# First-stage normalization with 97-row broadcasts and whole copies, and a final stage in fixed order with row factors from GpSimd

## The chip, the core and the metric

The kernel runs on one core of one Trainium2 chip. The metric is the device time of one execution in microseconds (us). The engines are TensorE (PE; its weight loads are listed as PEld), VectorE (DVE), ScalarE (ACT), GpSimd (POOL) and SyncE (SP), which issues most of the DMAs. PE works out of SBUF and writes into PSUM, which has eight banks of 128 x 512 floats here.

## What is computed

One decoder block on 512 tokens of width 1024, in float32. The parts that matter here are the first lines and the last:

```
hN = x * rsqrt(mean(x*x) + 1e-6) * norm_g
p  = hN @ w_in                       # 8992 columns, split into many branches
...                                  # mLSTM branch ya, sparse-attention branch yb
merged = sigmoid(g_a) * (ya @ w_branch_a) + sigmoid(g_b) * (yb @ w_branch_b)
x   = x + merged @ w_out
out = x * rsqrt(mean(x*x) + 1e-6) * final_norm_g
```

## The kernel before

**Number format.** Every float32 operand of a product is split in two float32r parts: a high one (written by ACT, in places by POOL) and a low one, the difference, by DVE. A product is three matmuls: high x high, high x low, low x high (`hh`, `hl`, `lh` below). PE is given 3025 matmuls.

**Order.** A planner orders the instructions of each engine, except where the code fixes the order: an engine whose name is in the set `ordered` issues in the order of the code, and so does a single instruction that is wrapped in `keep`. All engines run their queues strictly in order; a waiting instruction holds what is behind it.

**First stage (L291 to L474).** The 512 tokens are four blocks of 128 rows, `xts[0]` to `xts[3]`. `norm_g` is one row, `grow` (L297); a float32 matmul of a row of ones with it spreads it over 128 partitions into two PSUM banks `gB` (L321 to L327). Ahead of these, nine matmuls of a tile of zeros into the bank `idle` are issued (`warm`, L305). For each block:

- `squares` (L347): ACT sums the squares; `factor` (L354): POOL adds epsilon and raises to the power -0.5 (`pow` with `mhalf`), which gives `rs[tb]`. `stats` is both.
- `transposed` (L385): per half of 512 columns, DVE multiplies the block by its factor and by `gB`, and PE transposes it in four pieces into a PSUM bank.
- `high` and `low` (L399, L402): ACT copies the bank to `hTh` (the high part of the transposed, normed input hT), DVE writes the difference to `hTl`.
- `some_of` or `mm3`: 24 matmuls per block against 288 columns of `w_in` ("small" columns: two V branches and the gates), loaded as `sraw` and split into `shi` and `slo` by `small_hi` (ACT or POOL) and `small_lo` (DVE), two of eight row groups at a time.
- `evacuate` (L376): ACT and DVE take the 288 sums out of PSUM.

PE, ACT and DVE are in `ordered` here; PE leaves it at L450, so that blocks 2 and 3 are placed by the planner. On POOL the split of the first two row groups, `small_hi(0, "p")`, is written ahead of the factor of block 1.

**Middle.** The first large product, tokens x 1024 columns of `w_in` for V, is done in Winograd's form (`winograd`, L529): seven products of quarters instead of eight. Its sums of token quarters are made by `token_sums` (L489), eight DVE additions which first rebuild the quarters from `hTh` and `hTl`, in the tile `gate`. Then follow many projections, the attention and the mLSTM, which the change does not touch.

**Final stage (L1369 to L1499).** `merged @ w_out` is again in Winograd's form. `product` issues a quarter product: two blocks of 128 rows, 12 matmuls each, into two banks; `hilo` splits weights. The last four are MS2 and MS3 (banks X, rows 2 and 3 in L and R), MS1 (banks Y: row 2, then row 3 in two halves of 256 columns) and MS4, which adds to the same banks Y and gives rows 0 and 1. "Row" here is a block of 128 tokens, L and R its two halves of 512 columns. For each row:

- `aside` (L1402): ACT copies a bank to `late`, and a POOL DMA adds it to `xo`, which holds x.
- `join` (L1408): DVE adds half a bank to `xo`. `joined` also lets ACT square and sum it and DVE multiply it by `fg` (final_norm_g).
- `part_sum` and `scale_out` (L1418, L1430): the factor is made by ACT (Ln, Exp) and refined by four small DVE instructions; then ACT scales L, DVE scales R, and both are stored.

PE is in `ordered` again from L1388 on; ACT and DVE are not (L1460), so the planner places the steps of the four rows between each other.

Of the kernel before, what the change touches and what calls it, by code (L numbers as in the profile page):

```python
# [62 lines left out]
def build(  # L63
# [227 lines left out]
    with tc.tile_pool(name="ph0", bufs=2, side="right") as p0, tc.tile_pool(  # L291
# [5 lines left out]
        grow = p0.tile([1, D], F32, name="grow", bufs=1)  # L297
        keep(nc.scalar.dma_start(grow, norm_g))
# [3 lines left out]
        dve.memset(f(zero), 0.0)  # L302
        idle = PO()
# [38 lines left out]
        epst = p0.tile([128, 1], F32, name="epst", bufs=1)  # L342
        pool.memset(epst, EPS)
# [10 lines left out]
        def factor(tb):  # L354
            v = p0.tile([128, 1], F32, name="v", tag="v", bufs=4)
            r = p0.tile([128, 1], F32, name="r", tag="r", bufs=4)
            rs.append(r)
            keep(pool.tensor_scalar(v, ssq[:, tb : tb + 1], EPS, None, OP.add))
            if tb == 0:
                keep(pool.tensor_tensor(v, v, ssq[:, NT : NT + 1], OP.add))  # L360
            keep(pool.tensor_tensor(r, v, mhalf[:, 0:1], OP.pow))
            yield

        def stats(tb):
            squares(tb)
            fac = factor(tb)
            next(fac)
            return lambda: next(fac, None)
# [14 lines left out]
        stats(0)()  # L383

        def transposed(tb, banks=None):  # L385
            xt, pts = xts[tb], []
            for hf in range(2):
                hs = slice(hf * 512, hf * 512 + 512)
                dve.scalar_tensor_tensor(xt[:, hs], xt[:, hs], rs[tb][:, 0:1], gB[hf], OP.mult, OP.mult)
                ps = banks[hf] if banks else PT()  # L390
                for k in range(4):
                    kk = hf * 4 + k
                    pe.transpose(ps[:, k * 128 : (k + 1) * 128], xt[:, kk * 128 : (kk + 1) * 128], ident)
                pts.append(ps.rearrange("p (k t) -> p k t", k=4))
            return pts

        blk = [slice(tb * 128, tb * 128 + 128) for tb in range(NT)]

        def high(pts, tb, hf):  # L399
            A(hTh[:, hf * 4 : hf * 4 + 4, blk[tb]], pts[hf], AF.Copy)  # L400

        def low(pts, tb, hf):  # L402
            ks = slice(hf * 4, hf * 4 + 4)
            dve.tensor_tensor(hTl[:, ks, blk[tb]], pts[hf], f(hTh[:, ks, blk[tb]]), OP.subtract)

        def some_of(ps, tb, kind, ks, start=False, stop=False):
            ks = list(ks)
            for k in ks:
                l = (hTl if kind == "lh" else hTh)[:, k, blk[tb]]
                r = (slo if kind == "hl" else shi)[:, k, :]  # L410
                pe.matmul(ps[:, :SW], l, r, start=start and k == ks[0], stop=stop and k == ks[-1])

        first = PP(), PP()
# [10 lines left out]
        low(pts0, 0, 0)  # L424
        low(pts0, 0, 1)
        high(pts1, 1, 0)
        high(pts1, 1, 1)
        small_lo(0)
        small_lo(2)
        low(pts1, 1, 0)  # L430
        low(pts1, 1, 1)
        small_hi(6, "p")
        small_hi(4, "a")
        stats(2)()
        some_of(first[0], 0, "hh", lo4, start=True)
        some_of(first[0], 0, "lh", lo4)
        some_of(first[1], 1, "hh", lo4, start=True)
        some_of(first[0], 0, "hh", hi4)
        some_of(first[0], 0, "lh", hi4)
        some_of(first[1], 1, "hh", hi4)  # L440
        some_of(first[0], 0, "hl", lo4)
        some_of(first[1], 1, "hl", lo4)
        some_of(first[1], 1, "lh", lo4)
        some_of(first[1], 1, "lh", hi4)
        pts = transposed(2)
        small_lo(6)
        small_lo(4)
        some_of(first[0], 0, "hl", (6, 7, 4, 5), stop=True)
        some_of(first[1], 1, "hl", (6, 7, 4, 5), stop=True)
        ordered.discard("pe")  # L450
# [3 lines left out]
        stats(3)()  # L454
        pts3 = transposed(3, (PS(), PS()))
        for tb in (2, 3):
            for hf in range(2):
                high(pts, tb, hf)
                low(pts, tb, hf)
            evacuate(tb - 2, first[tb - 2])  # L460
            pts, before = pts3, last if tb == 3 else None
            last = PP()
            mm3(
                last[:, :SW], lambda k: hTh[:, k, blk[tb]], lambda k: hTl[:, k, blk[tb]],
                lambda k: shi[:, k, :], lambda k: slo[:, k, :], range(ND),
            )
        vq = quarters(vview, ((0, 0), (1, 0)))
        w1 = hilo(vq[0, 0])
        evacuate(2, before)
        stream.fetch()  # L470
        vq.update(quarters(vview, ((0, 1), (1, 1))))
        evacuate(NT - 1, last)
# [16 lines left out]
    def token_sums():  # L489
        a, b, c, d = (gate[:, tb].rearrange("p (k t) -> p k t", k=4) for tb in range(NT))  # L490
        t = dve.tensor_tensor
        hl = lambda k: [f(x) for x in parts[k]]
# [150 lines left out]
    def angles():  # L643
# [68 lines left out]
        "P1": (step,), "t3": (job,), "t2": (job, load), "P2": (step,), "C11": (job, step),  # L712
        "w6": (job,), "P6": (ordered.clear,), "P7": (lambda: next(more, None),), "P4": (lambda: next(turn),), "P5": (lambda: next(turn, None),),
# [594 lines left out]
    with tc.tile_pool(name="fin", bufs=1, reuse_waits="tile") as fp:  # L1308
# [90 lines left out]
        fv = fp.tile([128, NT], F32, name="fv")  # L1399
# [8 lines left out]
        def join(tb, cs, bank):  # L1408
            xv = xo[:, tb, cs]
            dve.scalar_tensor_tensor(xv, bank, 0.5, xv, OP.mult, OP.add)  # L1410
            return xv

        def joined(tb, cs, bank, n):
            xv = join(tb, cs, bank)
            A(junk[:, tb * 2 + n % 2, : cs.stop - cs.start], xv, AF.Square, accum_out=fs[:, tb, n : n + 1])
            dve.tensor_tensor(xv, xv, fg[:, cs], OP.mult)

        def part_sum(tb, n):  # L1418
            v = fb[:, tb : tb + 1]
            if n > 1:  # L1420
                dve.tensor_tensor(fs[:, tb, 0:1], fs[:, tb, 0:1], fs[:, tb, 1:2], OP.add)
            dve.tensor_scalar(v, fs[:, tb, 0:1], 1.0 / D, EPS, OP.mult, OP.add)
# [3 lines left out]
        def left(tb, bank):  # L1426
            joined(tb, L, bank, 0)
            part_sum(tb, 1)

        def scale_out(tb, n, pieces):  # L1430
            part, v, r = fb[:, tb : tb + 1], fv[:, tb : tb + 1], fr[:, tb : tb + 1]
            last = fs[:, tb, n : n + 1]
            A(r, last, AF.Ln, bias=part, scale=1.0 / D)
# [88 lines left out]
```

## Time and profile before

| | us |
|---|---|
| median of 3 runs | 621.82 |
| lowest and highest | 621.22, 622.04 |
| profiled execution | 621.46 |
| its span (first to last instruction or transfer) | 619.7 |

The profile is that of one execution. Its page gives the busy time of each engine, slices of the span, the chain of work that ended last, and the costliest groups of instructions. The trace behind it can be asked for a timeline (start and duration of each instruction in us, engine, line, operation, output tile <- input tiles, shape, number of instructions merged, and in brackets the idle time before it and what ended that), for the waits of an engine in total, and for busy times in given stretches. Almost all instructions carry line 79, that of the helper which issues them, so they are told apart by tiles: `xt` is a block of x, `sq` the squares, `pt`, `pp`, `ps` and `po` PSUM banks, `wh` and `wl` the parts of weights. A matmul's duration includes its pipeline's end, so the spacing of starts tells more than the duration. In a stretch view the last numbers are the granted PE clock, the share of the DMA engines and GB/s.

### The profile page before, as it was taken

To read this page: it belongs to the slowest core of one execution; us is meant where nothing else is said; L and a number is where in the kernel's file an instruction comes from. 1 tells how busy PE (TensorE), PEld (TensorE's weight loads), DVE (VectorE), ACT (ScalarE), POOL (GpSimd) and SP (SyncE) were. 2 spreads that over 40 slices of the span, in tenths; PEclk is the share of its full clock that TensorE was granted. 3 is DMA by queue.
4 is the path that set the end of the run, shared out by engine and by line. 5 is a ranking of instruction groups with operands and counts; after the bars stand their busy time and mean duration, and the time that the engine had idled before them with its cause. 6 is when DMAs were issued, how large, how long until landed. Compare 5 with 4: busy or idle time off the path is not lost.

```text
span 619.7 us, 8625 instructions
## 1 busy us (share of the span) xinstructions
PE 605.0 (98%) x3025; PEld 504.6 (81%) x3025; DVE 494.0 (80%) x962; ACT 343.5 (55%) x644; POOL 55.1 (9%) x114
## 2 busy tenths in 40 slices
PE   7999999999999999999999999999999999999995
PEld 5988888888888878787878887888787878888884
DVE  4799989497587587876967777789898997589986
ACT  5555556555452356556666575565656563434565
POOL 2100000000000002122112212000000000010120
PEclk9999999999999999999999999999999999999998
DMA  7944653502059252223132312432233224891624
GB/s 222 359 136 137 219 155 95 175 20 85 18 142 241 69 137 68 69 70 102 35 85 70 86 42 82 133 102 69 68 103 103 68 91 132 296 248 31 204 51 154
DMA packets 82811, 73.92 MB, mean 119 GB/s; under 512 B 4896, under 2 KB 64452, under 8 KB 82768
## 3 DMA queue, kind: packets, MB, share of 16 engines
q1 hardware_dynamic: 81470, 70.48, 38.0%
q0 software_dynamic: 1152, 2.62, 2.3%
q8 instruction: 24, 0.39, 0.3%
q10 hardware_dynamic: 146, 0.27, 0.1%
q14 instruction: 19, 0.16, 0.1%
HBM read 61.30 MB, written 8.39 MB: 112 GB/s over the span
## 4 chain that ended last, share of the span: by engine, by line
PE 76%; DVE 14%; ACT 3%; issue 3%; DMA 2%; POOL 1%; SPq 0%; POOLq 0%; ACTq 0%; DVEq 0%
PE pp L79 45%; PE ps L79 17%; PE pt L79 10%; PE po L79 3%; DVE u L79 3%; DVE wl L79 2%; ACT wh L79 1%; DMA sraw<-w_in 1%; DVE xo L79 1%; DVE Th L79 1%; DVE num L79 1%; DVE P L79 1%; DMA wr<-w_in 1%; DVE qkl L79 1%; ACT P L79 1%
## 5 line engine op out<-in xcount | busy, mean ns | idle before, releaser
L79 PE MATMUL pp<-hTh,wh 128*128 128x512 f32 (+1 forms) x360 | 142.9, 397 | 0.0
L79 PE MATMUL pp<-hTl,wh 128*128 128x512 f32 (+1 forms) x360 | 139.9, 389 | 0.0
L79 PE MATMUL pp<-hTh,wl 128*128 128x512 f32 (+1 forms) x360 | 139.6, 388 | 0.0
L79 ACT ACTIVATE wh<-wr 128x1024 fp32r<-128x1024 f32 x56 | 59.1, 1058 | 55.8 <-PE pp L79 45.5
L79 PEld LDWEIGHTS pp<-hTh,wl 128*128 128x128 f32 x360 | 67.8, 188 | 13.2
L79 DVE TENSOR_TENSOR wl<-wr,wh 128x1024 fp32r<-128x1024 f32 x56 | 68.1, 1217 | 10.9 <-ACT wh L79 10.8
L79 PEld LDWEIGHTS pp<-hTh,wh 128*128 128x128 f32 x360 | 67.8, 188 | 10.6
L79 PEld LDWEIGHTS pp<-hTl,wh 128*128 128x128 f32 x360 | 67.9, 189 | 9.8
L1035 POOL TENSOR_SCALAR P<-P,st 128x128 f32<-128x128 f32 (+1 forms) x64 | 34.4, 556 | 161.2 <-DVE st L79 126.6
L79 DVE TENSOR_TENSOR wl<-T,wh 128x1024 fp32r<-128x1024 f32 x28 | 33.8, 1221 | 11.3 <-ACT wh L79 11.3
L79 DVE TENSOR_TENSOR ptl<-pt,pth 128x512 fp32r<-128x512 f32 (+1 forms) x64 | 29.9, 485 | 14.5 <-ACT pth L79 14.0
L79 ACT ACTIVATE pth<-pt 128x512 fp32r<-128x512 f32 (+1 forms) x64 | 26.7, 433 | 26.2 <-PE pt L79 14.4
L79 ACT ACTIVATE P<-P,st 128x128 f32<-128x128 f32 (+3 forms) x64 | 35.5, 555 | 10.3 <-DVE st L79 9.9
L79 DVE TENSOR_TENSOR wl<-R,wh 128x1024 fp32r<-128x1024 f32 x28 | 33.7, 1219 | 9.1 <-ACT wh L79 9.1
L79 DVE CUSTOM_DVE_ANT_0 P<-ps,cst 128x128 f32<-128x128 f32 (+3 forms) x64 | 30.5, 486 | 12.5 <-PE ps L79 12.1
L79 DVE SCALAR_TENSOR_TENSOR u<-pp,prm,u 128x511 f32<-128x511 f32 (+2 forms) x48 | 35.6, 742 | 0.4 <-ACT u L79 0.2
L79 ACT ACTIVATE wh<-R 128x1024 fp32r<-128x1024 f32 x28 | 29.3, 1057 | 11.7 <-PE pp L79 4.3
L79 ACT ACTIVATE wh<-T 128x1024 fp32r<-128x1024 f32 x28 | 29.0, 1054 | 11.1 <-PE ps L79 6.4
L79 PE MATMUL ps<-k,Th 128*128 128x256 f32 (+2 forms) x112 | 29.1, 341 | 0.9 <-DVE st L79 0.4
L79 PE MATMUL pt<-cst,P 128*128 128x128 f32 x160 | 28.3, 277 | 1.5 <-DVE ptl L79 1.4
L79 PEld LDWEIGHTS pt<-cst,P 128*128 128x128 f32 x160 | 19.7, 140 | 11.5 <-DVE ptl L79 6.5
L79 PE MATMUL pp<-yah,wh 128*128 128x512 f32 x64 | 25.0, 391 | 0.0
(360 smaller groups left out, 1379.5 us busy)
## 6 DMA issues: line engine op xcount, KB each, us to landing
wr<-w_in SPq DMA_DIRECT2D x44, 512.0 KB, 4.1
R<-w_in SPq DMA_DIRECT2D x24, 512.0 KB, 5.0
gD<-sg SPq DMA_DIRECT2D x16, 256.0 KB, 2.0
s<-gD SPq DMA_DIRECT2D x16, 256.0 KB, 3.0
wr<-w_branch_a SPq DMA_DIRECT2D x8, 512.0 KB, 4.6
R<-w_out SPq DMA_DIRECT2D x8, 512.0 KB, 6.9
vD<-cq SPq DMA_DIRECT2D x8, 256.0 KB, 2.1
wr<-vD SPq DMA_DIRECT2D x4, 512.0 KB, 4.3
```

The lines of the kernel that those rows point to most:

```text
L79: ins = fn(*args, **kw)
L1035: pool.tensor_scalar(pj, pj, st[:, 2, j : j + 1], 1.0, OP.mult, OP.mult)
```

## The change

Three parts.

1. **First stage.** `grow` and `one` become tiles of 128 partitions; norm_g is loaded into partition 96, DVE clears partitions 0 to 95, and the two broadcasts are matmuls of 97 rows. Zero matmuls are added after them (6), after the first half of block 0's transposes (3) and after the second (4, where 2 stood). `stats(1)` is written ahead of `small_hi(0, "p")`, so block 1's factor stands ahead of that split on POOL. The order of the rest is written out for all four blocks, and PE stays in `ordered` until all 96 small matmuls are issued.
2. **Token sums.** A new step `whole` lets ACT copy each transposed bank also to `gate`, unsplit (8 copies of 128x512). `token_sums` then needs four DVE additions, in place. One stream job and the second step of `token_sums` are written after the split of w6, no longer before it.
3. **Final stage.** ACT and DVE go back into `ordered` after the matmuls of MS3, and all steps are written out in a fixed order: each row is joined, squared, its factor made, scaled and stored. The factor is made by POOL (`begin` and `more` add up epsilon and the sums, `factor` raises to -0.5). One of the copies through `late` and a DMA (row 3) is a `join` with -0.5 instead. In rows 2 and 3, and in parts of rows 0 and 1, DVE multiplies by the factor and by `fg` in one instruction (`both`).

```diff
-        grow = p0.tile([1, D], F32, name="grow", bufs=1)
-        keep(nc.scalar.dma_start(grow, norm_g))
+        grow = p0.tile([128, D], F32, name="grow", bufs=1)
+        keep(nc.scalar.dma_start(grow[96:97, :], norm_g))
...
+        dve.memset(grow[:96, :], 0.0)
...
-        one = p0.tile([1, 128], F32, name="one", bufs=1)
+        one = p0.tile([128, 128], F32, name="one", bufs=1)
...
-            pe.matmul(ps, one, grow[:, hf * 512 : hf * 512 + 512], start=True, stop=True)
+            pe.matmul(ps, one[:97], grow[:97, hf * 512 : hf * 512 + 512], start=True, stop=True)
             gB.append(ps)
+        warm(6)
...
+        def whole(tb, hf):
+            q = gate[:, tb // 2 * 2 + hf].rearrange("p (k t) -> p k t", k=4)
+            A(q[:, :, tb % 2 * 128 : tb % 2 * 128 + 128], banks[tb, hf], AF.Copy)
...
+        normed(0, 0)
+        turned(0, 0, PT())
+        warm(3)
+        normed(0, 1)
+        turned(0, 1, PT())
+        stats(1)
         small_hi(0, "p")
-        pts0 = transposed(0)
-        after = stats(1)
-        high(pts0, 0, 0)
+        high(0, 0)
+        high(0, 1)
         small_hi(2, "a")
-        high(pts0, 0, 1)
-        after()
-        warm(2)
-        pts1 = transposed(1, (PP(), idle))
+        warm(4)
+        low(0, 0)
+        normed(1, 0)
+        turned(1, 0, PP())
+        some_of(0, "hh", lo4)
+        normed(1, 1)
+        turned(1, 1, idle)
+        low(0, 1)
+        small_hi(6, "p")
+        high(1, 0)
+        high(1, 1)
+        small_hi(4, "a")
...
+        whole(0, 0)
+        whole(0, 1)
+        stats(2)
...
+        whole(1, 0)
+        whole(1, 1)
+        stats(3)
...
+        for tb in (3, 2):
+            for hf in (1, 0):
+                whole(tb, hf)
+        for tb in (2, 3):
+            some_of(tb, "hh", lo4)
...
     def token_sums():
...
-        t(a, *hl("A21"), OP.add)
-        t(b, a, hl("A22")[0], OP.subtract)
-        t(b, b, hl("A22")[1], OP.subtract)
-        t(c, *hl("A11"), OP.add)
-        t(a, c, a, OP.subtract)
-        t(c, b, c, OP.subtract)
-        t(d, c, hl("A12")[0], OP.add)
-        t(d, d, hl("A12")[1], OP.add)
+        t(a22, a21, a22, OP.subtract)
+        t(a21, a11, a21, OP.subtract)
+        t(a11, a22, a11, OP.subtract)
+        t(a12, a11, a12, OP.add)
...
-        "P1": (step,), "t3": (job,), "t2": (job, load), "P2": (step,), "C11": (job, step),
-        "w6": (job,), "P6": (ordered.clear,), ...
+        "P1": (step,), "t3": (job,), "t2": (job, load), "P2": (step,), "w6": (job, step, job),
+        "P6": (ordered.clear,), ...
...
+        def more(tb, n):
+            v = fb[:, tb : tb + 1]
+            keep(pool.tensor_tensor(v, v, fs[:, tb, n : n + 1], OP.add))
+        def factor(tb, n):
+            more(tb, n)
+            keep(pool.tensor_tensor(fr[:, tb : tb + 1], fb[:, tb : tb + 1], mhalf[:, 0:1], OP.pow))
...
+        ordered.update(("act", "dve"))
...
         product(Y[:1], "MS1", w5, tbs=(0,))
+        join(2, R, Y[0])
+        square(2, R, 1)
+        times(3, L)
+        begin(3)
+        factor(2, 1)
+        for n, cs in enumerate((R0, R1)):
+            product((None, Y[1 + n]), "MS1", w5, tbs=(1,), cs=halves_of[n])
+            join(3, cs, Y[1 + n][:, halves_of[n]])
+            square(3, cs, 1 + n)
+            if n == 0:
+                more(3, 1)
+                scaled(2, L)
+                both(2, R)
+                store(2, R)
+        factor(3, 2)
+        scaled(3, L)
+        both(3, R)
+        store(3, R)
         product(Y[:1], "MS4", w3, False, tbs=(0,))
+        join(0, R, Y[0])
+        square(0, R, 1)
+        product((None, Y[1]), "MS4", w3, False, tbs=(1,), cs=halves_of[0])
+        join(1, R0, Y[1][:, halves_of[0]])
+        square(1, R0, 1)
+        factor(0, 1)
+        more(1, 1)
+        times(1, R0)
+        scaled(0, L)
+        product((None, Y[2]), "MS4", w3, False, tbs=(1,), cs=halves_of[1])
+        join(1, R1, Y[2][:, halves_of[1]])
+        square(1, R1, 2)
+        both(0, R)
+        store(0, R)
+        factor(1, 2)
+        scaled(1, L, nc.scalar)
+        both(1, R1)
+        dve.tensor_scalar(xo[:, 1, R0], xo[:, 1, R0], fr[:, 1:2], None, OP.mult)
+        store(1, R)
```

`normed` and `turned` are the two halves of the old `transposed`; `scaled` is ACT's scaling and its store.

More of the change, by code (lines that the diff above doesn't have):

```diff
@@ L440, in build @@
[L440 to L445, printed above, removed]
+        low(1, 0)
+        low(1, 1)
+        some_of(0, "lh", lo4)
+        some_of(1, "hh", lo4)
+        some_of(0, "hh", hi4)
+        some_of(0, "lh", hi4)
+        some_of(1, "hh", hi4)
+        some_of(0, "hl", lo4)
+        some_of(1, "hl", lo4)
+        some_of(1, "lh", lo4)
@@ L453, in build @@
         nc.sync.dma_start(bng, b_nsa_gate[0].partition_broadcast(128))
-        stats(3)()
-        pts3 = transposed(3, (PS(), PS()))
+        for hf in range(2):
+            normed(2, hf)
+            turned(2, hf, PT())
+        three = idle, PS()
+        for hf in range(2):
+            normed(3, hf)
+            turned(3, hf, three[hf])
+        vq = quarters(vview, ((0, 0), (1, 0)))
         for tb in (2, 3):
             for hf in range(2):
[L458 to L467, printed above, removed]
-        w1 = hilo(vq[0, 0])
-        evacuate(2, before)
+                high(tb, hf)
+                low(tb, hf)
+            if tb == 2:
+                evacuate(0, sums[0])
+        w1 = hilo(vq[0, 0])
+        evacuate(1, sums[1])
+        for tb in (3, 2):
[3 more added lines that the diff above has]
+            some_of(tb, "hh", lo4)
+            some_of(tb, "hl", lo4)
+            some_of(tb, "hh", hi4)
+            some_of(tb, "hl", hi4)
+            some_of(tb, "lh", lo4)
+            some_of(tb, "lh", hi4, stop=True)
+        ordered.discard("pe")
+        evacuate(2, sums[2])
         stream.fetch()
         vq.update(quarters(vview, ((0, 1), (1, 1))))
-        evacuate(NT - 1, last)
+        evacuate(NT - 1, sums[3])
         sp.tile([128, 120], F32, name="pad")
@@ L1406, in aside, with join @@
                 pool.dma_start(xo[:, tb, j * 512 : j * 512 + 512], t, accum_op=OP.add)
-        def join(tb, cs, bank):
+        def join(tb, cs, bank, scale=0.5):
             xv = xo[:, tb, cs]
[L1410 to L1416, printed above, removed]
@@ L1428, in left @@
[L1428 to L1433, printed above, removed]
-            dve.scalar_tensor_tensor(v, last, 1.0 / D, part, OP.mult, OP.add)
-            A(r, r, AF.Exp, scale=-0.5)
-            dve.scalar_tensor_tensor(v, r, v, r, OP.mult, OP.mult)
-            dve.tensor_scalar(v, v, -0.5, 1.5, OP.mult, OP.add)
-            dve.tensor_tensor(r, r, v, OP.mult)
-            for cs, eng in pieces:
-                xv = xo[:, tb, cs]
-                if eng == "a":
-                    A(xv, xv, AF.Copy, scale=r)
-                else:
-                    dve.tensor_scalar(xv, xv, r, None, OP.mult)
-                queue = nc.scalar if eng == "a" and tb == 1 else nc.sync
-                queue.dma_start(out[0, tb * 128 : tb * 128 + 128, cs], xv)
+            join(tb, L, bank)
@@ L1448, in build @@
+            square(tb, L, 0)
+            times(tb, L)
+            begin(tb)
         X = [PS() for _ in range(2)]
@@ L1490, in build @@
-        joined(2, R, Y[0], 1)
-        scale_out(2, 1, ((L, "a"), (R, "d")))
-        list(row(3))
-        product(Y[:1], "MS4", w3, False, tbs=(0,))
-        joined(0, R, Y[0], 1)
-        scale_out(0, 1, ((L, "a"), (R, "d")))
-        last = row(1)
-        for n, cs in enumerate(halves_of):
-            product((None, Y[1 + n]), "MS4", w3, False, tbs=(1,), cs=cs)
-            next(last, None)
+        R0, R1 = slice(512, 768), slice(768, 1024)
+        join(2, L, X[0])
+        square(2, L, 0)
@@ new lines, in build @@
+        A(late[:, 4], X[0], AF.Copy, scale=-0.5)
+        pool.dma_start(xo[:, 2, R], late[:, 4], accum_op=OP.add)
+        times(2, L)
+        begin(2)
+        join(3, L, X[1])
+        w3 = [
+            tuple(wp.tile([128, 2, 512], F32R, name=t, tag=t, bufs=4) for t in ("wh", "wl"))
+            for _ in range(2)
+        ]
+        for (hi, _), q in zip(w3, b22):
+            A(hi, q, AF.Copy)
+        square(3, L, 0)
+        for (hi, lo), q in zip(w3, b22):
+            dve.tensor_tensor(lo, q, f(hi), OP.subtract)
+            if lo is w3[0][1]:
+                join(3, R, X[1], -0.5)
```

112 lines of the change are left out of this document (48 added, 64 removed).

## The prediction

> **What bounds the kernel now.** I read the page's busy shares first, then what TensorE (PE) waited for over the whole span, then the chain of waits at the start.
>
> ```profile
> PE 605.0 (98%) x3025; PEld 504.6 (81%) x3025; DVE 494.0 (80%) x962; ACT 343.5 (55%) x644; POOL 55.1 (9%) x114
> ```
>
> ```profile
> PE pp L79 <- DVE xt L79: 1.8, 1, 1.8
> PE pt L79 <- DVE ptl L79: 1.4, 4, 0.6
> ```
>
> ```profile
> 11.55 1.12 PE pp L79 x4
> ...
> 20.41 0.87 PE pt L79 x8
> ...
> 23.24 6.40 PE pp L79 x48
> 29.63 5.46 PE ps L79 x24
> ```
>
> PE is busy for 98%. Its longest wait is the 1.8 us that ends at 11.55; from there its matmuls follow each other to the last one at 611.90, and the next entry of the list is 1.4 us in four pieces. So the end is: when PE's dense work starts, how fast its first part runs, and the tail behind the last matmul. Work that the change adds to or takes from ScalarE (ACT), VectorE (DVE) or GpSimd (POOL) in between is worth nothing while PE stays fed.
>
> The timeline of the start:
>
> ```profile
> 1.32 2.29 PE L79 MATMUL po<-zero 128*128 128x256 f32 x9 [1.32 <-DVE lfs L79]
> 3.54 3.78 PE L79 MATMUL ps<-grow,one 1*128 1x512 f32 x4
> 6.65 1.06 ACT L79 ACTIVATE sq<-xt 128x1024 f32<-128x1024 f32 x1 [1.55 <-DMA xt<-x]
> 7.25 0.71 PEld L79 LDWEIGHTS pt<-cst,xt 128*128 128x128 f32 x4 [1.50 <-DVE xt L79]
> 8.40 0.60 ACT L79 ACTIVATE hTh<-pt 128x512 fp32r<-128x512 f32 x1 [0.61 <-PE pt L79]
> 9.07 0.68 POOL L336 TENSOR_SCALAR shi<-sraw 128x576 fp32r<-128x576 f32 x1 [2.97 <-DMA sraw<-w_in]
> 9.82 0.22 POOL L358 TENSOR_SCALAR v<-ssq 128x1 f32<-128x1 f32 x1
> 10.13 0.58 POOL L361 TENSOR_TENSOR r<-v,mhalf 128x1 f32<-128x1 f32 x1
> 10.74 1.41 DVE L79 SCALAR_TENSOR_TENSOR xt<-xt,r,ps 128x512 f32<-128x512 f32 x2 [2.58 <-POOL r L361]
> 11.24 0.67 POOL L336 TENSOR_SCALAR shi<-sraw 128x576 fp32r<-128x576 f32 x1 [0.53 <-DMA sraw<-w_in]
> 12.07 1.28 DVE L79 TENSOR_TENSOR hTl<-pt,hTh 128x512 fp32r<-128x512 f32 x2
> 13.17 1.31 PE L79 MATMUL pp<-shi,hTh 128*128 128x288 f32 x4
> 15.24 1.98 PE L79 MATMUL pp<-shi,hTh 128*128 128x288 f32 x8
> 18.12 1.23 PE L79 MATMUL pp<-slo,hTh 128*128 128x288 f32 x8
> 29.47 0.39 PE L79 MATMUL ps<-wh,hTh 128*128 128x512 f32 x1
> ```
>
> Two things are to be seen. First, block 1's squares are done at 7.8, but its factor on POOL stands behind a weight split that waits for a DMA until 9.07; so the factor comes at 10.7 and block 1's transposes at 11.55. Second, the clock: eight matmuls of 288 columns take 1.98 at 15.24 and 1.23 at 18.12, ends included, or 0.25 and 0.133 each (48 in 6.40). PE runs at half clock until about 16.9, though the slices print 9 there. Nine matmuls of zeros and 3.4 us of one-row matmuls did not raise it: the transposes at 7.25 still go at 0.18, against 0.11 (eight in 0.87) at 20.41.
>
> **Part 1, the first stage.** I added it up queue by queue, in program order, with the rows above. The same addition over the order of before gives 29.35 for the first Winograd matmul; measured is 29.47, so I add 0.1.
>
> When does the clock rise? Before, dense full-row work began at 11.55 and the clock rose at 16.9, 5.35 later; counted from the first 288-column matmul it is 3.75. The trace shows no 97-row matmul. If it counts like a full-row one, PE is dense from 1.32 and the clock rises between 5.1 and 6.7; I take 6.7, the longer count. The duration of a 97-row matmul is bounded by the one-row rows, 0.86 at half clock, and half of that: 3.54 to 6.96. The new clearing of `grow`, 96x1024, lies between a 0.38 memset of 384 columns and about 1.1 scaled up; it ends by 2.4, hidden before 3.54. If it had to wait for norm_g's landing, it would cost up to 1.0.
>
> Then: six warm matmuls at 0.12 to 7.7 (0.4 later than the transposes at 7.25, the price of the filling), block 0's transposes and three more to 8.9. On POOL block 1's factor now stands ahead of the split: squares end 7.8, factor 8.7. ACT copies block 0's banks 8.35 to 9.75, shi[2:4] to 10.3; DVE does block 0's first low part 9.0 to 9.7, then block 1's product to 10.3. Block 1's transposes start at 10.36 (11.55 before) and the first sums at 10.8 (13.17). PE waits once more, 12.8 to 13.2, for shi[4:6], which ACT makes after block 1's copies. From there 36 matmuls x 0.133 = 4.8 to 18.0; 16 transposes 1.75 plus 0.4 of waits for block 3's factor to 20.2 (ACT makes the squares of 2 and 3 between the new whole copies); 48 x 0.133 = 6.4 to 26.6. With the 0.1: 26.7 against 29.47, **2.75 gained**. The weights of that product are split on DVE by 25.8, so they wait for nothing. The eight whole copies (0.5 each) and the evacuations end by 28.3, beside PE. The loads of the three bias rows keep their place ahead of the weight quarters on SP, so no transfer moves. Of the 2.75, some 1.2 is the earlier start of block 1 and the rest the clock.
>
> **Part 2, the token sums.** Eight DVE additions become four:
>
> ```profile
> L79 DVE TENSOR_TENSOR gate<-gate,hTl 128x1024 f32<-128x1024 f32 x2 | 2.4, 1224 | 0.0
> ```
>
> Some 4.7 us of DVE go. PE had no wait there, so I cost it at 0; what it buys is cover for the start that now comes 2.75 earlier. The job moved behind w6 leaves PE's order of products and jobs the same.
>
> **Part 3, the end.**
>
> ```profile
> 603.52 0.87 POOL L1406 DMA_DIRECT2D xo<-late  x1 [2.13 <-ACT late L79]
> 604.58 0.68 DVE L79 SCALAR_TENSOR_TENSOR xo<-pp,xo 128x512 f32<-128x512 f32 x1
> 606.40 0.40 PE L79 MATMUL pp<-wh,mSh 128*128 128x512 f32 x1
> 606.87 0.42 DVE L79 SCALAR_TENSOR_TENSOR xo<-pp,xo 128x256 f32<-128x256 f32 x1 [1.60 <-DMA xo<-late]
> 611.90 0.28 PE L79 MATMUL pp<-wh,mSl 128*128 128x256 f32 x1
> 612.23 0.42 DVE L79 SCALAR_TENSOR_TENSOR xo<-pp,xo 128x256 f32<-128x256 f32 x1
> 613.15 0.42 ACT L79 ACTIVATE junk<-xo 128x256 f32<-128x256 f32 x1
> 614.40 0.30 ACT L79 ACTIVATE fr<-fs,fb 128x1 f32<-128x1 f32 x1
> 615.60 0.72 ACT L79 ACTIVATE xo<-xo,fr 128x512 f32<-128x512 f32 x1 [0.67 <-DVE fr L79]
> 616.35 0.38 ACTq L1446 DMA_DIRECT2D out<-xo  x1
> ```
>
> PE's last matmul ends at 612.18; the last scaling ends at 616.32, 4.14 later. The old factor takes from the last square, 613.66 with its accumulator read, to 615.60: 1.94 over two ACT and four DVE instructions. The new one is two POOL instructions; the first stage has their like:
>
> ```profile
> 5.25 0.19 POOL L360 TENSOR_TENSOR v<-v,ssq 128x1 f32<-128x1 f32 x1 [0.74 <-ACT sq L79]
> 5.51 0.58 POOL L361 TENSOR_TENSOR r<-v,mhalf 128x1 f32<-128x1 f32 x1
> 6.13 0.75 DVE L79 SCALAR_TENSOR_TENSOR xt<-xt,r,ps 128x512 f32<-128x512 f32 x1 [4.84 <-POOL r L361]
> ```
>
> 0.88 from the first to the reader, about 1.0 with the hand-over. But the fixed order puts each row's scaling ahead of the next row's join on DVE and ACT, so the four factors stand in one chain. From PE's own times: block 2's square ends 605.9, factor 606.9; DVE does block 2's scaling, then block 3's last join, 607.6 to 608.0, one us after its bank was full; square, factor 609.5; block 3's scaling, block 0's join to 610.8; factor 612.6; ACT scales block 0 to 613.3 while block 1's last join (612.8) waits; its square ends 613.75, factor 614.75, last scaling 615.5 on ACT and 615.4 on DVE. That is **0.85 before** 616.32. The stall at 606.87 goes with its DMA (block 3's part is a DVE join, 0.7). PE keeps its cover: block 2's last join ends at 605.2 and the second low weight at 604.6, both needed from 606.40 on, where the last products begin to add to the same banks. Bounds: POOL rows vary by 0.1, four in the chain, so 0.4 to 1.2.
>
> At these times POOL's power for row 0 (611.7 to 612.6) meets DVE's product by `fg`, both operands in SBUF. The Trainium skill, "SBUF — State Buffer", "Who interferes with whom", says that such a DVE instruction and a GpSimd one that reads SBUF shut each other out; no row here shows it. By it the sum would be about 0.2 poorer.
>
> **Sum.** The profiled execution took 621.46 (span 619.7 and 1.8 around it): 621.46 - 2.75 - 0.85 = 617.9. The median of the runs, 621.82, lies 0.36 above the profiled one; I say 618.0. Its own range: rise at 5.1 gives 0.6 more, at 8.1 0.65 less, the end 0.4 either way: 616.9 to 618.9.
>
> **Rivals.**
> - *Late rise.* The 97-row matmuls do not count as full; dense work begins at 6.96, and 5.4 later the clock rises, at 12.4. Everything to there runs at 0.25 and 0.18. First product at 28.35: 1.1 gained, 619.5. For it: one-row matmuls did nothing. Chance 0.17.
> - *The clock falls again.* From 6.7 to 13.5 PE has about 1.4 us of waits and four groups of four transposes. At the end of the run the clock fell 2.1 us after the last matmul (mean 0.63 in this slice, and 0.50 after it):
>
> ```profile
> 614.00:615.00 1.00, 0.00 (x0) 0.00 (x0) 0.74 (x5) 0.90 (x3) 0.00 (x0) 0.63 0.00 0
> ```
>
> My longest wait is 1.0, so I expect no fall; but if a third of idle time is enough, it falls at 10.1 and rises at 16.9 as before: first product at 28.9, 0.6 gained, 620.0. Chance 0.13. The Trainium skill, "TensorE: Matmul & The Clock Gate", "Part 4: PE-mode transpose", says that transposes do not count as PE-busy; by it this stretch would be busy for only 55%, and this rival is what it would give. The same page, "Part 1", has the clock rise after some 3.4 us of sustained work whatever it is; the trace disagrees, since PE was busy from 1.32 to 8.8 without a rise.
> - *It does not do what it says*: the clock rises at 16.9 as before. Filling and half clock eat the earlier start, 29.5 against 29.47; only the end is left: 620.6. Chance 0.10.
> - *Slower: the chain of four powers.* Each factor is waited for by DVE and ACT in order, so a factor longer by d moves the end by 4d. It eats its own gain from d = 0.2; the whole is slower by 1.24 (0.2%) from d = (2.75 + 0.85 + 1.24)/4 = 1.2. At d = 1.3 it gives 617.9 + 5.2 = 623.1. For it: POOL never made these beside a busy DVE in a trace shown here. Against it: its last DMA issue is over by 601.4, and 0.58 is a steady row. Chance 0.08, with every other way to lose.
>
> **How the numbers follow.** Forecast 0.52, late rise 0.17, fall 0.13, no rise 0.10, slower 0.08. Down to 620.4 the range leaves out the last two, 0.18. A measurement of this kernel tells about 0.2%, 1.24 us, from no change: faster 0.82, same 0.10, slower 0.08.
>
> **What would show it.** Right: 288-column sums at 0.133 from the first one on; block 1's transposes near 10.4; first Winograd matmul near 26.7, last matmul near 609.4; no PE wait in between; the last scaling 3.3 after the last matmul. Wrong: sums at 0.25 before 16.9; a PE wait behind `grow`; a PE wait in the last products for a join; factors over 1.1 in the tail.

## The result and the profile after

The changed kernel takes **618.03 us** (median of 6 runs, 617.80 to 618.76) against 621.53 for the kernel before on the same chip (6 runs, 620.70 to 622.04): a ratio of 0.9946, 95% interval 0.9934 to 0.9959. A second set of 5 runs gave 618.08 and the same ratio and interval (experiment 9). The forecast was 618.0. The profiled execution took 617.8, with a span of 615.78.

The busy shares of the page after, and what PE waited for (total, times, longest):

```profile
PE 602.1 (98%) x3036; PEld 502.7 (82%) x3036; DVE 488.5 (79%) x932; ACT 345.9 (56%) x643; POOL 59.3 (10%) x126
```

```profile
PE pp L79 <- DVE xt L79: 0.8, 1, 0.8
```

PE issues eleven matmuls more than before and is yet busy for 2.9 us less, since fewer of its matmuls run at half clock; the wait of 1.8 ahead of block 1 is now 0.8. The timeline of the start:

```profile
3.40 3.14 PE L79 MATMUL ps<-grow,one 97*128 97x512 f32 x4
5.97 1.28 PE L79 MATMUL po<-zero 128*128 128x256 f32 x6
7.09 0.60 PE L79 MATMUL pt<-cst,xt 128*128 128x128 f32 x4
8.20 0.57 POOL L362 TENSOR_TENSOR r<-v,mhalf 128x1 f32<-128x1 f32 x1
9.06 0.68 POOL L339 TENSOR_SCALAR shi<-sraw 128x576 fp32r<-128x576 f32 x1 [0.29 <-DMA sraw<-w_in]
9.76 0.66 PE L79 MATMUL pp<-cst,xt 128*128 128x128 f32 x4 [0.81 <-DVE xt L79]
10.17 0.78 PE L79 MATMUL pp<-shi,hTh 128*128 128x288 f32 x4
25.98 0.40 PE L79 MATMUL ps<-wh,hTh 128*128 128x512 f32 x1
```

The first four sums take 0.78, ends included, where before 0.25 each was seen until 16.9: PE is at full clock. In the trace's clock records it rises at 5.94 (16.93 before). Block 1's factor (8.20) stands ahead of the split (9.06), so its transposes start at 9.76 (11.55 before) and the first Winograd matmul at 25.98 (29.47 before). The tail:

```profile
608.32 0.28 PE L79 MATMUL pp<-wh,mSl 128*128 128x256 f32 x1
608.53 0.55 POOL L1454 TENSOR_TENSOR fr<-fb,mhalf 128x1 f32<-128x1 f32 x1
609.12 0.72 ACT L79 ACTIVATE xo<-xo,fr 128x512 f32<-128x512 f32 x1 [0.53 <-POOL fr L1454]
609.75 0.40 ACT L79 ACTIVATE junk<-xo 128x256 f32<-128x256 f32 x1
610.65 0.55 POOL L1454 TENSOR_TENSOR fr<-fb,mhalf 128x1 f32<-128x1 f32 x1
611.23 0.72 ACT L79 ACTIVATE xo<-xo,fr 128x512 f32<-128x512 f32 x1 [1.00 <-POOL fr L1454]
611.64 0.35 DVE L79 TENSOR_SCALAR xo<-xo,fr 128x256 f32<-128x256 f32 x1
611.99 0.40 ACTq L1457 DMA_DIRECT2D out<-xo  x1
```

Row 0's factor releases ACT at 609.12, ACT's square of row 1 has to wait behind that scaling until 609.75, and so on to the last scaling, which ends at 611.99. From the start of the last matmul this is 3.67; before it was 616.32 - 611.90 = 4.42. The stores of the two ends, issue to landing (median for SP's seven, the one of ACT's queue), first of the kernel before, then of the changed one:

```profile
out<-xo SPq DMA_DIRECT2D x7, 256.0 KB, 2.2
out<-xo ACTq DMA_DIRECT2D x1, 256.0 KB, 2.5
```

```profile
out<-xo SPq DMA_DIRECT2D x7, 256.0 KB, 2.5
out<-xo ACTq DMA_DIRECT2D x1, 256.0 KB, 2.8
```

So the span splits like this:

| stretch | before | after | gain | forecast |
|---|---|---|---|---|
| start to first Winograd matmul | 29.47 | 25.98 | 3.49 | 2.75 |
| from there to the last matmul | 582.43 | 582.34 | 0.09 | 0 |
| last matmul's start to the end of the last scaling | 4.42 | 3.67 | 0.75 | 0.85 |
| from there to the end of the span | 3.36 | 3.79 | -0.43 | 0 |
| outside the span | 1.78 | 2.02 | -0.24 | 0 |
| sum (profiled executions) | 621.46 | 617.80 | 3.66 | 3.60 |

The sum came out within 0.06, and that closeness is luck, because two errors cancel: the start gained 0.74 more than forecast, and the last three rows gave 0.77 less. The 0.24 outside the span is not the end's doing: the time of a run less its span is about 2.0 in every run of the changed kernel and about 1.8 in those of the kernel before, but also 1.8 in the runs of experiments 2 and 7, which have the new end. What makes it is open.

**How the clock moves.** From rise to fall the clock records of the two profiles show 614.26 - 16.93 = 597.33 and 613.51 - 5.94 = 607.57 us, 175.0 and 178.0 times 3.4133, and in all 14 profiles such times are whole numbers of this step. So the clock is decided at the points of a grid of 3.4133 us, which lies differently against the kernel's start in each execution. The Trainium skill, "TensorE: Matmul & The Clock Gate", "Part 1", describes such a free-running window of 3413 ns; the trace agrees, and it fits that the runs of one kernel spread by 1.0 us (after) or 2.7 us (before, 620.32 to 623.04 over 24 runs).

### The profile page after: what moved, and what is told of

It is laid out like the page before. It is cut to its first block, busy times and chain, and to the rows that moved or that the text cites. A ratio compares the mean times of both kernels' runs of the same rounds, so it can differ in the third digit from the quotient of the medians.

```text
span 615.8 us, 8634 instructions
## 1 busy us (share of the span) xinstructions
PE 602.1 (98%) x3036; PEld 502.7 (82%) x3036; DVE 488.5 (79%) x932; ACT 345.9 (56%) x643; POOL 59.3 (10%) x126
## 4 chain that ended last, share of the span: by engine, by line
PE 76%; DVE 14%; ACT 4%; issue 2%; DMA 1%; POOL 1%; SPq 0%; POOLq 0%; DVEq 0%; ACTq 0%
PE pp L79 44%; PE ps L79 18%; PE pt L79 10%; PE po L79 3%; DVE u L79 3%; DVE wl L79 2%; ACT wh L79 1%; DVE P L79 1%; ACT P L79 1%; DMA xt<-x 1%; DVE xo L79 1%; DVE ptl L79 1%; DVE Th L79 1%; DVE num L79 1%; DMA wr<-w_in 1%
## 5 line engine op out<-in xcount | busy, mean ns | idle before, releaser
L79 ACT ACTIVATE wh<-R 128x1024 fp32r<-128x1024 f32 x28 | 29.3, 1058 | 16.2 <-PE pp L79 6.5
```

The costliest lines, as they stand in the source:

```text
L79: ins = fn(*args, **kw)
```

## The experiments

Twelve runs. "Rise" is the clock record's first rise; "tail" runs from the last matmul's start to the end of the last scaling; ratios are to the kernel before on the same chip.

| run | rise | first Winograd matmul | tail | median (range) | ratio, 95% interval |
|---|---|---|---|---|---|
| before | 16.93 | 29.47 | 4.42 | 621.53 (620.70 to 622.04) | |
| after | 5.94 | 25.98 | 3.67 | 618.03 (617.80 to 618.76) | 0.9946 (0.9934 to 0.9959) |
| 1 one row | 11.20 | 28.05 | 3.66 | 620.30 (620.19 to 620.74) | 0.9977 (0.9968 to 0.9986) |
| 2 no filling | 5.48 | 26.38 | 3.66 | 618.63 (617.63 to 619.60) | 0.9956 (0.9941 to 0.9971) |
| 3 old end | 6.34 | 26.57 | 5.28 | 619.43 (619.11 to 619.63) | 0.9963 (0.9950 to 0.9976) |
| 4 joins first | 7.63 | 26.78 | 3.03 | 617.83 (617.65 to 618.28) | 0.9941 (0.9926 to 0.9956) |
| 5 split first | 4.80, 15.04 | 29.13 | 3.66 | 621.15 (619.92 to 622.38) | 0.9992 (0.9982 to 1.0003) |
| 6 slow factor | 7.53 | 26.73 | 5.05 | 619.48 (619.17 to 619.89) | 0.9975 (0.9965 to 0.9985) |
| 7 eight sums | 7.48 | 26.42 | 3.65 | 618.64 (618.37 to 619.30) | 0.9962 (0.9948 to 0.9976) |
| 8 rows only | 17.88 | 30.18 | 4.41 | 621.44 (620.35 to 622.52) | 0.9998 (0.9988 to 1.0008) |
| 9 changed again | 5.12 | 26.14 | 3.65 | 618.08 (617.75 to 618.66) | 0.9946 (0.9934 to 0.9959) |
| 10 joins again | 7.55 | 26.75 | 3.03 | 617.96 (617.37 to 618.07) | 0.9941 (0.9927 to 0.9955) |
| 11 65 rows | 5.12 | 26.43 | 3.65 | 619.21 (618.18 to 619.23) | 0.9960 (0.9945 to 0.9975) |
| 12 end only | 17.74 | 30.14 | 3.65 | 621.26 (620.59 to 622.26) | 0.9997 (0.9988 to 1.0006) |

In the profiles with the new start, 16.2 us pass from block 1's first transpose to the first Winograd matmul (17.52 in run 5, where the clock falls, and 15.93 in run 7, which has no whole copies); in those with the old start, 17.9 to 18.0. What else differs between the profiles with the new start lies ahead of that transpose.

### 1: the changed kernel with a one-row broadcast

```diff
-            pe.matmul(ps, one[:97], grow[:97, hf * 512 : hf * 512 + 512], start=True, stop=True)
+            pe.matmul(ps, one, grow[:, hf * 512 : hf * 512 + 512], start=True, stop=True)
```

> The changed kernel with the broadcasts back to one row (norm_g in partition 0, no clearing). Theory (a matmul of one row does not count for the clock, one of 97 rows does): the clock no longer rises near 6 us but only after full-row work from about 7 us on, between 10.3 and 13.7; the first 288-column sums go at 0.25 each; first Winograd matmul at 27.6 to 28.8 instead of 26.0; 1.2 to 2.2 us slower than the changed kernel. Rival (the added zero matmuls raise the clock, the rows do not matter): rise near 6 us as in the changed kernel, and the same time within 0.4.

Its timeline:

```profile
3.53 3.78 PE L79 MATMUL ps<-grow,one 1*128 1x512 f32 x4
7.24 1.65 PE L79 MATMUL po<-zero 128*128 128x256 f32 x6
8.69 1.05 PE L79 MATMUL pt<-cst,xt 128*128 128x128 f32 x4
9.39 0.99 PE L79 MATMUL po<-zero 128*128 128x256 f32 x3
10.18 1.05 PE L79 MATMUL pt<-cst,xt 128*128 128x128 f32 x4
11.81 0.66 PE L79 MATMUL pp<-cst,xt 128*128 128x128 f32 x4
```

Here four transposes still take 1.05; the clock rises at 11.20, and only block 1's go in 0.66. It costs 2.3 us against the changed kernel. The grid lies almost as in run 4: a window from 4.37 to 7.79 here does not raise the clock, one from 4.21 to 7.63 there does, with 97-row matmuls in it. So the one-row matmuls, busy as they look, leave the clock down, and the 97-row ones bring it up. The window that raised the clock here, 7.79 to 11.20, holds some 1.4 us of transposes (8.69 to 9.39, 10.18 to 10.89). Without them it would be busy for 59%. The Trainium skill, "TensorE: Matmul & The Clock Gate", "Part 4: PE-mode transpose", says that transposes do not count as PE-busy in the same way. Either they do count here, or 59% of a window is enough. No run settles which: the 65% of a window that raised nothing (11.05 to 14.47 in run 8, shown there) are mostly transposes themselves.

### 2: the changed kernel without the added filling

```diff
-        warm(6)
...
-        warm(3)
...
-        warm(4)
+        warm(2)
```

> The changed kernel without the added zero matmuls (6 and 3 taken out, 2 instead of 4), 97 rows kept. Theory (the rows raise the clock; gaps shorter than 2 us do not lower it): rise between 5 and 8 us, no fall, 288-column sums at 0.133 from the first on, block 0's transposes up to 0.7 earlier; first Winograd matmul within 0.4 of 26.0, time within 0.5 of the changed kernel. Rival (without filling the clock falls again): sums at 0.25 between 10 and 13.5 or 17, first Winograd matmul at 27.5 or later, 1.5 to 2.5 slower.

The runs fall into two groups: 617.63, 617.79 and 617.98, and 619.28, 619.28 and 619.60. The profile (617.98) is of the first: clock up at 5.48, and it stays up over a PE wait of 1.93 us, in a grid window that is busy for 63% (the columns are explained under run 5):

```profile
8.89:12.31 3.42, 2.16 (x18) 2.16 (x19) 3.42 (x6) 2.09 (x4) 1.73 (x3) 1.00 1.04 333
```

That the other three lost the clock in a window that held more of the wait fits two of them by the mean granted clock listed for each run (619.28 at 0.995, 619.28 at 0.993; the first group has 0.997 and 0.998). It does not fit the third, 619.60 at 0.997; a later first rise would, as the time ahead of the first rise is listed as 1.00. No profile of any of the three was taken. So the filling costs nothing where the grid is kind, and is worth some 1.5 us where it is not; by which of the two ways is not shown.

### 5: block 1's factor behind the split again

```diff
-        stats(1)
         small_hi(0, "p")
+        stats(1)
```

> The changed kernel with block 1's squares and factor put back behind the weight split of GpSimd that waits for a DMA (as the kernel before has it); the 97 rows, the filling and the end stay. If the earlier place of block 1's factor is worth what the prediction says (1.2 of the 2.75 us): block 1's transposes at about 10.9 to 11.5 instead of 9.76, the first Winograd matmul at about 27.1, the time 0.8 to 1.2 above the changed kernel's 618.0, so 619.0. Rival, the place is worth nothing because PE waits anyway at 12.65 for ScalarE's part of the weights: first Winograd matmul at 26.0 to 26.3, time 618.0 to 618.3. The clock should rise at its first grid point after 4.7 in either case.

Measured 621.15, 3.1 above the changed kernel; both forecasts were far off. The stretch view by the grid of this execution (length, busy time of PE, PEld, DVE, ACT, POOL with counts; then granted clock, DMA share, GB/s; it prints 1.00 also ahead of the first rise):

```profile
4.80:8.21 3.41, 3.04 (x19) 2.21 (x18) 1.41 (x2) 1.90 (x5) 0.76 (x2) 1.00 1.10 299
8.21:11.63 3.42, 0.78 (x8) 0.58 (x6) 1.51 (x3) 1.37 (x3) 1.78 (x4) 1.00 1.14 319
11.63:15.04 3.41, 3.41 (x15) 3.39 (x16) 3.12 (x5) 1.06 (x2) 0.37 (x1) 0.50 0.37 126
15.04:18.45 3.41, 3.41 (x26) 3.25 (x26) 2.03 (x3) 3.41 (x8) 0.52 (x2) 1.00 0.99 378
```

```profile
PE pp L79 <- DVE xt L79: 2.6, 1, 2.6
```

PE waits 2.6 us for block 1, the window 8.21 to 11.63 is busy for only 0.78 of 3.42, and the clock falls for the whole next window, although PE is fully busy in it. That is the rival "the clock falls again", for want of the earlier factor. The factor's place is worth 29.13 - 25.98 = 3.15 in this execution: 1.85 of transposes that start later (11.61 against 9.76), and 1.3 of half clock behind them. Not every execution has the fall. Three of the ten runs (619.92, 620.25 and 620.36) list a mean granted clock of 0.997, and a window at half clock (0.003 of the run) beside the half clock at the run's end (0.0015 or more in every profile) would leave 0.996 at most. They are still 1.9 to 2.3 above the changed kernel, about what the later transposes cost.

### 8: the kernel before with the 97-row broadcast alone

```diff
-            pe.matmul(ps, one, grow[:, hf * 512 : hf * 512 + 512], start=True, stop=True)
+            pe.matmul(ps, one[:97], grow[:97, hf * 512 : hf * 512 + 512], start=True, stop=True)
```

> The kernel before with nothing changed but the 97-row broadcast of norm_g (and its cleared rows). If the row count alone brings the clock: rise at a grid point between 4.7 and 8.2, block 1's transposes at about 11.5 as before, the sums at 0.133 from the first one on; if the clock stays up over the waits before 11.55 the first Winograd matmul is at about 27.2 to 27.7 instead of 29.47 and the time 1.8 to 2.2 below the kernel before. Rival, without filling the clock falls again in the waits of 8 to 11.5: sums at 0.25 at first, first Winograd matmul at 28.5 to 29.4, time 0 to 1 below before. Which of the two comes may hang on where the grid lies, so that single runs spread over both.

With it go the tiles of 128 partitions and the clearing of `grow`, as in the change. Nothing was gained: 621.44 against 621.46, ratio 0.9998 (0.9988 to 1.0008). The grid window 4.23 to 7.64 did not raise the clock, though PE is listed as busy for 3.37 of its 3.41:

```profile
4.23:7.64 3.41, 3.37 (x7) 1.25 (x6) 1.27 (x2) 1.15 (x5) 1.00 (x3) 1.00 0.97 304
...
11.05:14.47 3.42, 2.23 (x10) 2.23 (x11) 3.03 (x5) 0.82 (x2) 1.03 (x2) 1.00 0.58 218
```

```profile
7.06 1.98 PE L79 MATMUL pt<-cst,xt 128*128 128x128 f32 x8
12.24 1.12 PE L79 MATMUL pp<-cst,xt 128*128 128x128 f32 x4 [2.77 <-DVE xt L79]
```

PE's starts leave some 0.24 us free between the broadcasts and the transposes at 7.06, and the matmuls have 97 rows of 128. Then it waits for block 1, and the next chance is a window that begins after 12.24. So in this execution the rows alone do not bring the clock, and over ten runs they gain nothing; in the changed kernel the six zero matmuls close that gap, and the earlier factor the next one. The parts of the first stage do not add up. By the first Winograd matmul in one profile each, the rows without the rest gain nothing (30.18 against 29.47), the rest without the rows 1.4 (28.05), all together 3.5 (25.98).

### 11: 65 rows instead of 97

```diff
-            pe.matmul(ps, one[:97], grow[:97, hf * 512 : hf * 512 + 512], start=True, stop=True)
+            pe.matmul(ps, one[:65], grow[:65, hf * 512 : hf * 512 + 512], start=True, stop=True)
```

> The changed kernel with norm_g broadcast over 65 rows instead of 97; filling, order and end stay. If any count of rows well above one is full work: clock up by 8.2, first Winograd matmul at 25.9 to 26.9, time 617.7 to 618.8 as with 97 rows. Rival, a window's work is weighted by its rows and the clock wants some 0.77 of a full window (the one profile with 97 rows and 0.24 us of idle time, 0.74 by that weight, did not rise; 0.79 and more did): 65 rows give 0.51 to 0.80, so in most executions the clock rises one window later, at 8.3 to 11.7, first Winograd matmul at 27.2 to 28.1, time 619.3 to 620.4, near that of the one-row kernel.

One run took 618.18, as with 97 rows; its profile has the rise at 5.12, in a window half of which were full-row matmuls. The other three took 619.20 to 619.23, above every one of the 11 runs with 97 rows (617.75 to 618.76). So the number of rows still matters between 65 and 97. A weight by rows fits all profiles: full-row time plus 97/128 or 65/128 of the rest makes 0.74 of the window that did not raise the clock in run 8, 0.75 of the one that did here, and 0.79 in run 3. But it rests on two profiles close to the limit, and no profile was taken of the three late runs, so it is not settled.

### 6: one more GpSimd instruction ahead of each power

```diff
+            v = fb[:, tb : tb + 1]
+            keep(pool.tensor_scalar(v, v, 1.0, None, OP.mult))
             keep(pool.tensor_tensor(fr[:, tb : tb + 1], fb[:, tb : tb + 1], mhalf[:, 0:1], OP.pow))
```

> The changed kernel with one further GpSimd instruction of 128x1 (a multiplication by 1.0, about 0.2 busy and 0.3 with its hand-over) ahead of each row's power in the end. If the four factors stand in one chain: the piece from the start of the last matmul to the end of the last scaling grows from 3.63 by about 1.2, or the last matmul comes later by a part of it, and the time is about 619.2. Rival, only the last factor counts because the others have slack behind PE: that piece grows by 0.3, time 618.3.

```profile
612.50 0.22 POOL L1455 TENSOR_SCALAR fb<-fb 128x1 f32<-128x1 f32 x1
612.81 0.57 POOL L1456 TENSOR_TENSOR fr<-fb,mhalf 128x1 f32<-128x1 f32 x1
613.41 0.72 ACT L79 ACTIVATE xo<-xo,fr 128x512 f32<-128x512 f32 x1 [1.33 <-POOL fr L1456]
613.81 0.34 DVE L79 TENSOR_SCALAR xo<-xo,fr 128x256 f32<-128x256 f32 x1
```

The power starts 0.31 later than it could (612.50 to 612.81). The tail grows from 3.67 to 5.05, by 1.38: four times 0.31 and a little, not once. The time follows, 619.48. The four factors do stand in one chain.

### 3 and 12: the old end behind the new start, and the new end behind the old start

Run 3 is the changed kernel with the final stage of the kernel before, of which the core is:

```diff
-        ordered.update(("act", "dve"))
...
-            keep(pool.tensor_tensor(fr[:, tb : tb + 1], fb[:, tb : tb + 1], mhalf[:, 0:1], OP.pow))
...
+            A(r, last, AF.Ln, bias=part, scale=1.0 / D)
...
+        aside(X, 2, 1, 1, -0.5)
```

> The changed kernel with the final stage of before. Theory (end and start are worth 0.8 and 2.7 to 3.5, and simply add): start as in the changed kernel, 4.4 us from the last matmul's start to the end of the last scaling instead of 3.6, 0.5 to 1.1 us slower than the changed kernel. Rival (the end's gain is eaten by what follows the last scaling): the same time within 0.3.

It lost 1.4 us against the changed kernel; the tail is 5.28, not 4.42:

```profile
604.80 0.42 DVE L79 SCALAR_TENSOR_TENSOR xo<-pp,xo 128x256 f32<-128x256 f32 x1 [2.46 <-DMA xo<-late]
```

In the kernel before this wait for the adding DMA was 1.60. The wait is longer by 0.86, as is the tail. The last adding transfer ran for 2.40 us here (602.05 to 604.45 in the transfer records) and for 1.52 there. One of its 144 packets, begun at 602.64, took 0.86 us, where no other took more than 0.24; the last six then come late, one behind the other. What held that packet is not shown; a load of 16 KB of instructions had run from 601.02 to 602.50. The new end has no such transfer in row 3. Without the 0.86 the loss would be some 0.5 us, an estimate that takes all five runs to have it; one was profiled.

Run 12 is the kernel before with the new final stage, the same diff the other way round.

> The kernel before with the new end alone. If the end is worth its 0.85 on its own: tail 3.6 to 3.7 instead of 4.41, 0.7 to 0.9 below the kernel before less 0.4 for the last store's landing in the profile, so 620.7 against 621.5. Rival, behind the late first stage the joins meet the adding transfers in other places and nothing is gained: 621.3 to 621.6. The first Winograd matmul stays at 28.9 to 30.2.

The tail is 3.65, as in the changed kernel, so the end does the same behind either start. But the time is 621.26, ratio 0.9997 (0.9988 to 1.0006): no gain that these runs can tell, though the interval leaves room for up to 0.7 us, and the median of the kernel before in this set is 621.84. Part of the gain goes behind the last scaling. In the three profiles with the old end, 3.36 us pass from there to the end of the span; in those with the new end, 3.67 to 3.90. The transfer records show where: counted from the end of the last scaling, SP's last packet of the kernel before lands at 1.46 and the store of ACT's queue runs nearly alone, 0.84 long, to 2.14; in the changed kernel both halves are stored at 612.0, SP's packets run to 2.21, and ACT's store takes 1.28, to 2.39. Of the 0.43, 0.25 is thus two stores side by side. DVE's half used to be done at 616.08, 0.24 ahead of ACT's; the new end gives DVE two instructions there (611.24 and 611.64), so it ends with ACT's. No kernel was run that stores it sooner, so this cause is read from the records alone.

### 7: the eight token sums again

```diff
-        whole(0, 0)
-        whole(0, 1)
...
-        t(a22, a21, a22, OP.subtract)
+        t(a, *hl("A21"), OP.add)
+        t(b, a, hl("A22")[0], OP.subtract)
+        t(b, b, hl("A22")[1], OP.subtract)
...
```

> The changed kernel with the eight additions of halves (high and low parts) of the kernel before instead of the whole copies and four additions in place. The prediction costs this part at 0: from the first Winograd matmul to the last matmul 582.3 to 582.6 as in every kernel so far, first Winograd matmul 25.7 to 26.4 (ScalarE has eight copies less), time 617.7 to 618.4. Rival, the 4.7 us of VectorE that the four additions save carry the earlier start: PE waits for a sum behind the first products and the middle grows by 1 to 2.5 us, time 619 to 620.5.

Neither side: the middle grew to 583.09, by 0.7 against the changed kernel's 582.34, while the first Winograd matmul came 0.3 earlier than in runs with the same rise (26.42 against 26.73 and 26.75), since ACT has eight copies less. Half of it is one wait:

```profile
42.07 2.35 DVE L79 TENSOR_TENSOR wl<-R,wh 128x1024 fp32r<-128x1024 f32 x2
43.34 0.50 PE L79 MATMUL pp<-wl,hTh 128*128 128x512 f32 x1 [0.19 <-DVE wl L79]
```

DVE splits this weight behind its last additions, at 42.07, and PE, which could start at 42.99, waits until 43.34. In the changed kernel DVE is at that weight at 39.50, and PE does not wait:

```profile
39.50 2.35 DVE L79 TENSOR_TENSOR wl<-R,wh 128x1024 fp32r<-128x1024 f32 x2
```

So part 2 is cover, worth about 0.4 net by these profiles; the medians differ by 0.6, with intervals that overlap. Not all of the middle's growth need be part 2's: the middle is 582.84 and 582.85 in runs 1 and 5, which have part 2, mostly because one wait for DVE (tile `st`) takes 0.75 there instead of 0.40.

### 4, 9 and 10: a version with two joins ahead of a scaling

```diff
             if n == 0:
                 more(3, 1)
-                scaled(2, L)
-                both(2, R)
-                store(2, R)
+        scaled(2, L)
+        both(2, R)
+        store(2, R)
         factor(3, 2)
```

> The changed kernel with row 2's scalings (L on ScalarE, R on VectorE, and the store) written behind row 3's last join and square. Theory (the four factors stand in one chain because each row's scaling waits for its power ahead of the next row's join): row 3's factor comes about 0.9 earlier, row 0's join no longer waits for row 3's scaling, and the last scaling ends 3.0 after the start of the last matmul instead of 3.6: 0.5 to 0.7 faster than the changed kernel. Rival (the tail hangs on the last matmul alone): no change within 0.3.

> The changed kernel itself, beside the next one on the same chip: 617.7 to 618.8, median 618.1; the clock up by 8.2 and no fall, the tail (start of the last matmul to the end of the last scaling) 3.65.

> The changed kernel with row 2's scalings and store moved behind row 3's last join and square. In a single profile the tail was 3.03 instead of 3.66. If the tail decides: 0.6 below the changed kernel, so 617.5 with a tail of 3.0, and the interval of the one lies below the median of the other. Rival, row 2's later store keeps the queue of the stores busy and gives the gain back behind the last scaling: time as the changed kernel, 617.9 to 618.2.

The tail is 3.03 in both profiles, 0.64 less, as expected from taking one scaling out of the chain. The time moves less: 617.96 beside 618.08 in the same set, 617.83 in the first; the intervals (0.9927 to 0.9955 and 0.9934 to 0.9959) overlap, so the two are not told apart. Both profiles of this version have a late rise (7.55 and 7.63, the first Winograd matmul 0.6 to 0.8 later than in the changed kernel's two profiles), and 0.1 goes behind the last scaling again (3.86 and 3.90 to the end of the span). It beats the kernel before; that it beats the changed one is not shown.

## Why the prediction was right, step by step

- **What bounds the kernel.** Right. From the first Winograd matmul to the last, 582.2 to 583.1 us pass in every profile, whatever was done at the two ends.
- **Part 1, the rise of the clock.** The likeliest case came true: matmuls of 97 rows bring the clock and those of one row do not (run 1), with a gap or fewer rows as the limit (runs 8 and 11). The step that failed is the size: the rise was put at 6.7, from two lengths of dense work in one profile, 5.35 and 3.75. There is no such length. The clock is decided on the grid, and profiles of kernels with the whole start of part 1 rise between 5.12 and 7.63. Behind block 1's transposes the addition held: 16.3 to the first Winograd matmul was forecast (10.36 to 26.7), 16.2 was measured. Of the extra gain of 0.74, 0.60 lies ahead of them, as they start at 9.76. In runs 4, 6 and 10, with the rise at 7.53 to 7.63, they start at 10.51 to 10.56 and the first Winograd matmul comes at 26.73 to 26.78, as forecast; so much of the extra gain is luck of where the grid lay. The rise alone does not fix it either: at 5.12 (run 9) the first Winograd matmul comes at 26.14, later than at 5.94. That the trace disagrees with a rise after sustained work of any kind stands, for one-row matmuls (run 1). The free-running window that the Trainium skill, "TensorE: Matmul & The Clock Gate", "Part 1", describes was not used in the forecast, and the two profiles' 175.0 and 178.0 steps agree with it.
- **Part 1, the place of block 1's factor.** The forecast took 1.2 of the 2.75 for the earlier start and the rest for the clock, as if they could be added. The profile after has 1.79 (11.55 to 9.76) and 1.70 (17.92 to 16.22 behind it). But run 5 shows that they cannot be had one by one: with the factor back, the clock falls in its profile, and 3.15 of the 3.49 are gone. Run 8 shows it from the other side. "The price of the filling", 0.4 on block 0's transposes, was not paid in the profile, where they start at 7.09 (7.25 before); with a rise at 7.53 they start at 7.85, so the price hangs on the grid.
- **Part 2.** Costed at 0, with the remark that it is cover for the earlier start. Right: nothing in the middle moved, and without it the wait appears (run 7).
- **Part 3.** The tail gained 0.75 for 0.85, and the chain of four factors is real (run 6). What failed is a term that the prediction put at nothing without a reason: what follows the last scaling. It grew by 0.43, of which two stores side by side are 0.25. How much of the end's gain reaches the clock is not settled: alone it gained nothing that can be told (run 12, at most 0.7), and taking it back behind the new start cost 1.4, 0.86 of it by a slower transfer (run 3).
- **Rivals.** *Late rise* and *does nothing* did not happen; run 1 is what the first would have been (620.3 measured, 619.5 forecast). *The clock falls again* shows in none of the 11 runs of the changed kernel (at most 618.76), but it is near: run 5 has it, and two of run 2's slower three fit it. *The chain of four powers* is right as a mechanism and 4d as its price; d stayed at 0, as the powers took 0.55 to 0.58 as before. The 0.2 that the prediction estimated from the Trainium skill, "SBUF — State Buffer", "Who interferes with whom", for DVE and GpSimd shutting each other out did not show in the tail of the changed kernel. In the tail of runs 4 and 10 one addition on GpSimd, beside a DVE product of two SBUF tiles, takes 0.43 instead of 0.19.

## What to carry to other kernels

Before a change that is to bring the clock up earlier, list the windows of the clock's grid that it could fall on, and look for the one with the least work: here the wider matmul gained nothing alone, and with the filling and the earlier operand 3.5 us. Undo parts of such a change one at a time before any of them is called useless. And follow an end's gain to the landing of the last store: two halves that finish at the same time can share what one of them had to itself.

## What the runs showed of the hardware that was not expected

- The clock's grid of 3.4133 us holds inside a kernel as well: in run 5 it rises at 4.80, falls at 11.63 and rises at 15.04, two and one steps apart. A window does not have to be idle for a fall: those with 39% (the end of the kernel before) and 23% (run 5) of PE work were followed by half clock, those with 46% (the end of run 7) and 63% (run 2) were not.
- A matmul's listed busy time does not tell how it counts for the clock. Windows listed as busy for 99% or more did not raise it, once mostly of one-row matmuls (run 1, 4.37 to 7.79) and once of 97 rows with 0.24 us free between starts (run 8).
- DVE and GpSimd held each other up where both read SBUF. In the changed kernel two splits on DVE meet one on GpSimd:

```profile
10.88 1.89 DVE L79 TENSOR_TENSOR slo<-sraw,shi 128x576 fp32r<-128x576 f32 x2
13.89 1.41 DVE L79 TENSOR_TENSOR slo<-sraw,shi 128x576 fp32r<-128x576 f32 x2
```

```profile
11.23 0.94 POOL L339 TENSOR_SCALAR shi<-sraw 128x576 fp32r<-128x576 f32 x1 [1.49 <-DMA sraw<-w_in]
```

The first pair takes 1.89 instead of the second's 1.41, and the split 0.94 instead of the 0.68 that it takes at 9.06. The Trainium skill, "SBUF — State Buffer", "Who interferes with whom", states this for a DVE instruction with two SBUF inputs; the rows agree. It cost nothing here, as PE was not waiting for these splits.
